# Attention probabilities turned by VectorE and DMA instead of TensorE, with four engines in the program's order

## The chip, the core and the metric

One NeuronCore of a Trainium2 chip runs the whole program. The metric is the device time of one execution in microseconds; three runs of the kernel before gave 835.94, 836.59 and 836.82 us, a median of 836.59. A profile of one execution shows when each instruction ran on TensorE (PE), VectorE (DVE), ScalarE (ACT) and GpSimd (POOL); SyncE (SP) issues DMAs.

## The reference

Two layers on 512 tokens of width 1024, each behind an RMS norm and added to the residual, and a final RMS norm: a state-space mixer (layer 0), then latent attention with 16 heads (layer 1), which the change touches. Cut to that:

```python
proj = u @ in_w
c_q, c_kv, k_r, z = proj[..., :384], proj[..., 384:640], proj[..., 640:704], proj[..., 704:]
q = (rms_norm(c_q, q_norm_w) @ uq_w).reshape(bsz, seq, 16, 192)
kv = (rms_norm(c_kv, kv_norm_w) @ ukv_w).reshape(bsz, seq, 16, 128 + 128)
q_full = concat([q[..., :128], rope(q[..., 128:])])
k_full = concat([kv[..., :128], rope(k_r) for every head])
s = einsum('bqhd,bkhd->bhqk', q_full, k_full) * 192 ** -0.5       # causal
o = einsum('bhqk,bkhd->bqhd', softmax(s), kv[..., 128:])
y = (o.reshape(bsz, seq, 2048) * silu(z)) @ out_w
return rms_norm(h + y, final_norm_w)
```

## The kernel before

All is float32. For accuracy each operand of a large matmul is kept as a high part, rounded to the fast format (`a`, `qh`, `ph`, `whi`, written by a ScalarE cast), and a rest (`b`, `ql`, `pl`, `wlo`, written by a VectorE subtraction that reads the high part); a product is three matmuls, the last with one of the rests. So each tile that feeds TensorE passes ScalarE and then VectorE.

Layer 0 (`ssm`, up to some 425 us of the span) is the same in both kernels. `mla` then computes the first projection, norms, and the 16 heads.

- `front_a(j)` and `front_b(j)` project q, k, v and the rope part for heads 2j and 2j+1. `front_a` runs under even heads (with rope: three VectorE steps, two ScalarE casts and two VectorE rests; the two halves of the rope tile are swapped by four DMAs into `rsw`), `front_b` under odd heads (with v). `zgemm(i)` projects the gate of head i.
- `score(h, b)` multiplies q-block b (128 tokens) with all keys up to it, takes the masked minimum on VectorE, the exponential with its sum on ScalarE, then the reciprocal and the scaling on VectorE: probabilities p, with queries on partitions.
- `turn(h, kb)` brings keys onto partitions: one 128x128 transpose on TensorE for each query block from kb on (4 + 3 + 2 + 1 per head, L817), then the cast `ph` (L821) and the rest `pl` (L822).
- `product(h, kb)` multiplies v with them: (va, ph), (vb, ph), (va, pl), 512, 384, 256 and 128 wide. After the fourth the result is multiplied with the gate.
- `zsilu(m)` applies the silu to four gates; ScalarE loads another function table before and the exponential's again after.
- `out_tok` multiplies with the output weights, for the first 8 heads while the last heads run.

What sets the order: TensorE's queue is the program's order. `sched(feed, pieces)` walks through the projections of a head (`feed`, which yields after about six matmuls with their cost) and puts in each score, turn and product once the fed cost passes its place; places are the tables SF (head 0's scores), SC (scores of head h+1 under head h), TU and PR (turns and products of head h), as shares of the head's cost. On all other engines a scheduler decides the order before. Every engine works through its queue in order: an instruction that waits holds up those behind it. Weights come through two raw buffers and three of each part; `weight` splits one weight ahead of the one in use (`LOOK`).

Of the kernel before, what the change touches and what calls it, by code (L numbers as in the profile page):

```python
# [15 lines left out]
P = 128  # L16
# [34 lines left out]
OA = 8  # L51
SQ = 2

# [98 lines left out]
class Net:  # L152
# [8 lines left out]
    def build(self):  # L161
# [18 lines left out]
        self.phase, self.group, self.before, self.head = "", [], [], None  # L180
        self.wq = []
        self.wpos = self.wload = 0
        self.wraws = []
        self.wready = {}
        for g in range(NG):
            for i in range(6):
                self.wq.append(("w", U_IN + 6 * g + i))
# [18 lines left out]
        with tc.tile_pool(name="ps_m", bufs=1, space=bass.MemoryType.PSUM, reuse_waits="tile") as ps, \  # L206
                tc.tile_pool(name="mla", bufs=2, reuse_waits="tile") as wk:
            self.ps, self.wk = ps, wk
            self.mla()

    LOOK = 1

    def link(self, ins, others):
        for o in others:
# [3 lines left out]
    def E(self, out, in_, func, **k):  # L218
        if self.phase != "E":
            pre = self.nc.scalar.preload_act_table_set("natural_log_exp_and_others")  # L220
            self.link(pre, self.group)
            self.phase, self.group, self.head = "E", [pre], pre
        i = self.nc.scalar.activation(out, in_, func, **k)  # L223
# [13 lines left out]
    def sched(self, feed, pieces=()):  # L237
        pieces = sorted(pieces, key=lambda p: p[0])
        done = 0.0
        for cost in feed:  # L240
            done += cost
            while pieces and pieces[0][0] <= done:
                pieces.pop(0)[1]()
# [3 lines left out]
    def weight(self, kind, idx):  # L247
        key = (kind, idx)
        self.prefetch(self.wq.index(key) + 1 + self.LOOK)
        return self.wready.pop(key)  # L250

    def prefetch(self, want):
        while self.wload < min(want + 1, len(self.wq)):
            self.wraws.append(self.load_weight(*self.wq[self.wload]))
            self.wload += 1
        while self.wpos < min(want, len(self.wq)):
            self.wready[self.wq[self.wpos]] = list(self.split_weight(self.wraws.pop(0)))[-1]
            self.wpos += 1

    def load_weight(self, kind, idx):  # L260
        n = {"w": 1024, "ua": 1024, "ub": 640, "uc": 512}[kind]
        raw = self.wraw.tile([P, n], F32, tag="raw", name=self.nm("raw"))
        self.nc.sync.dma_start(raw[:], self.t[kind][idx])
        return raw

    def split_weight(self, raw, cuts=()):
# [4 lines left out]
        for a, b in zip((0, *cuts), (*cuts, n)):  # L271
            nc.scalar.copy(hi[:, a:b], raw[:, a:b])  # L272
            nc.vector.tensor_tensor(lo[:, a:b], raw[:, a:b], hi[:, a:b].bitcast(F32), op=ALU.subtract)  # L273
# [29 lines left out]
    def run(self, g):  # L303
        for _ in g:
            pass
# [54 lines left out]
    def ssm(self):  # L360
# [45 lines left out]
        for i, w in enumerate(ws):  # L406
            self.wready[self.wq[i]] = next(w)
# [242 lines left out]
    def mla(self):  # L650
        tc, nc, t, wk = self.tc, self.nc, self.t, self.wk
        v = nc.vector
        self.bufs = {"b": 8}
        col = lambda i: self.cols[:, i:i + 1]
# [16 lines left out]
        for i in range(6):  # L671
# [6 lines left out]
            if i >= 2:  # L678
                for k in (2 * i - 4, 2 * i - 3):
                    ht = wk.tile([P, T], F32, tag=("ph", "pl")[k % 2], name=self.nm("ht"))  # L680
# [11 lines left out]
        def rope(raw):  # L692
# [11 lines left out]
        F = [{} for _ in range(8)]  # L704
# [10 lines left out]
        def zsilu(m):  # L715
            for i in range(4 * m, 4 * m + 4):
                self.S(zt[i][:], zt[i][:])

        def ksplit(src):
            k = wk.tile([P, 2, T], F32R, tag="k", name=self.nm("k"))  # L720
            nc.scalar.copy(k[:, 0], src)
            v.tensor_tensor(k[:, 1], src, k[:, 0].bitcast(F32), op=ALU.subtract)
            return k

        def front_a(j):
# [6 lines left out]
            rot = rope(raw)  # L732
            s1 = wk.tile([P, T], F32R, tag="s1", name=self.nm("s1"), bufs=1)
            s2 = wk.tile([P, T], F32R, tag="s2", name=self.nm("s2"), bufs=2)
            nc.scalar.copy(s1[lo, :], rot[lo, :])
            nc.scalar.copy(s2[hi, :], rot[hi, :])
            v.tensor_tensor(s1[hi, :], rot[lo, :], s1[lo, :].bitcast(F32), op=ALU.subtract)
            v.tensor_tensor(s2[lo, :], rot[hi, :], s2[hi, :].bitcast(F32), op=ALU.subtract)
            f["r", 0], f["r", 1] = s1, s2
# [3 lines left out]
            f["q", 0] = self.split(ps[:], "q", wk)  # L743
# [3 lines left out]
            f["k", 0] = ksplit(ps[:])  # L747
            yield 1.3

        def front_b(j):  # L750
# [4 lines left out]
            f["q", 1] = self.split(ps[:], "q", wk)  # L755
# [3 lines left out]
            f["k", 1] = ksplit(ps[:])  # L759
# [3 lines left out]
            for half in range(2):  # L763
# [13 lines left out]
                v.tensor_tensor(vb[:], ps[:], va[:].bitcast(F32), op=ALU.subtract)  # L777
# [3 lines left out]
        probs = [[] for _ in range(MH)]  # L781

        def score(h, b):
            f, i = F[h // 2], h % 2
            (qa, qb), kk = f["q", i], f["k", i]
# [285 lines left out]
```

## Time and profile before

| | us |
|---|---|
| the profiled execution | 836.13 |
| its span | 834.0 |
| busy in the span: TensorE, VectorE, ScalarE, GpSimd | 819.3, 644.9, 450.4, 0.2 |
| median of three runs | 836.59 |

The page says how long each engine was busy in the span of the execution; "idle before" a group is time in which its engine waited, and the name behind the arrow is what ended the wait. The granted clock of TensorE was 0.999 over the span. 50,856 DMA packets moved 90.55 MB, 21,552 of them under 512 bytes. All DMAs but a few are issued by SyncE.

### The profile page before, as it was taken

The page shows a single profiled execution, that of the slowest core. Times are in us where ns is not written, and L with a number is a line of the kernel's source. Part 1 is how long each engine was busy: PE and PEld are TensorE (multiplying, and loading weights), DVE is VectorE, ACT ScalarE, POOL GpSimd, SP SyncE. Part 2 cuts the span into 40 slices and gives each one's busy share as a digit, 9 for nine tenths or more (in the row PEclk, how much of TensorE's full clock was granted, in tenths as well). Part 3 has the DMA queues.
Part 4 walks back from the last instruction along what each step waited for, and adds up shares of the span by engine and source line. Part 5 has one row for each costly group of instructions (what it writes and reads, how often), then busy time and mean ns, then how long its engine had stood idle before and what let it go on. Part 6 is the DMA issues. An engine that isn't in the chain of part 4 may idle for free.

```text
span 834.0 us, 11549 instructions
## 1 busy us (share of the span) xinstructions
PE 819.3 (98%) x4228; PEld 691.8 (83%) x4228; DVE 644.9 (77%) x1234; ACT 450.4 (54%) x794; POOL 0.2 (0%) x4
## 2 busy tenths in 40 slices
PE   7999999999999999999999999999999999999996
PEld 5887888888888888888888888888888888888885
DVE  7999898979787989778566787786767869675544
ACT  7567755545465657434353654556547557554233
POOL 0000000000000000000000000000000000000000
PEclk9999999999999999999999999999999999999999
DMA  6364543423242423333555142222222224331212
GB/s 227 103 191 141 155 147 106 152 99 129 101 139 90 152 76 127 115 121 94 130 130 132 54 130 64 79 72 76 63 64 58 90 78 152 101 97 56 86 66 101
DMA packets 50856, 90.55 MB, mean 109 GB/s; under 512 B 21552, under 2 KB 23088, under 8 KB 50800
## 3 DMA queue, kind: packets, MB, share of 16 engines
q1 hardware_dynamic: 50080, 88.77, 34.0%
q10 hardware_dynamic: 720, 1.05, 0.3%
q8 instruction: 33, 0.54, 0.3%
q14 instruction: 23, 0.19, 0.1%
HBM read 83.12 MB, written 4.33 MB: 105 GB/s over the span
## 4 chain that ended last, share of the span: by engine, by line
PE 92%; DVE 3%; DMA 2%; ACT 1%; SPq 1%; issue 0%; DVEq 0%; ACTq 0%
PE mm L291 55%; PE ot L941 11%; PE s L793 5%; PE mm L300 4%; PE po L835 4%; PE mm L773 3%; PE pt L817 2%; PE yd L138 2%; PE yd L291 1%; PE aux L130 1%; PE aux L105 1%; DMA x<-in_x_dram 1%; PE aux L77 1%; PE aux L89 1%; DMA L<-ac_d 1%; DVE wlo L273 1%
## 5 line engine op out<-in xcount | busy, mean ns | idle before, releaser
L272 ACT CAST whi<-raw 128x1024 fp32r<-128x1024 f32 (+3 forms) x132 | 127.0, 965 | 210.3 <-PE mm L291 172.8
L273 DVE TENSOR_TENSOR wlo<-raw,whi 128x1024 fp32r<-128x1024 f32 (+3 forms) x132 | 146.8, 1115 | 54.6 <-ACT whi L272 54.3
L291 PE MATMUL mm<-ah,whi 128*128 128x512 f32 x384 | 154.0, 401 | 0.0
L291 PE MATMUL mm<-ah,wlo 128*128 128x512 f32 x384 | 150.3, 391 | 0.4 <-DVE wlo L273 0.4
L291 PE MATMUL mm<-al,whi 128*128 128x512 f32 x384 | 149.9, 390 | 0.0
L291 PE MATMUL mm<-vh,whi 128*128 128x512 f32 x224 | 89.4, 399 | 0.8 <-ACT whi L272 0.8
L291 PE MATMUL mm<-vh,wlo 128*128 128x512 f32 x224 | 87.9, 392 | 0.7 <-DVE wlo L273 0.7
L291 PE MATMUL mm<-vl,whi 128*128 128x512 f32 x224 | 87.6, 391 | 0.0
L291 PEld LDWEIGHTS mm<-ah,wlo 128*128 128x128 f32 x384 | 72.1, 188 | 16.1 <-DVE wlo L273 0.8
L291 PEld LDWEIGHTS mm<-ah,whi 128*128 128x128 f32 x384 | 72.2, 188 | 15.3 <-issue 1.4
L291 PEld LDWEIGHTS mm<-al,whi 128*128 128x128 f32 x384 | 72.2, 188 | 14.4 <-DVE al L312 0.3
L941 PE MATMUL ot<-whi,ah 128*128 128x512 f32 (+1 forms) x136 | 52.4, 385 | 0.0
L941 PE MATMUL ot<-whi,al 128*128 128x512 f32 (+1 forms) x136 | 51.5, 379 | 0.0
L941 PE MATMUL ot<-wlo,ah 128*128 128x512 f32 (+1 forms) x136 | 51.4, 378 | 0.0
L291 PEld LDWEIGHTS mm<-vh,wlo 128*128 128x128 f32 x224 | 42.1, 188 | 10.7 <-DVE wlo L273 1.5
L291 PEld LDWEIGHTS mm<-vh,whi 128*128 128x128 f32 x224 | 42.2, 188 | 9.4 <-ACT whi L272 1.1
L223 ACT ACTIVATE p<-p,st 128x128 f32<-128x128 f32 (+1 forms) x64 | 36.1, 564 | 25.3 <-DVE st L805 25.2
L291 PEld LDWEIGHTS mm<-vl,whi 128*128 128x128 f32 x224 | 42.2, 188 | 7.3
L821 ACT CAST ph<-pt 128x512 fp32r<-128x512 f32 (+1 forms) x64 | 26.4, 421 | 33.3 <-PE pt L817 32.8
L291 PE MATMUL mm<-ch,whi 128*128 128x512 f32 x104 | 42.6, 410 | 0.0
L291 PE MATMUL mm<-ch,wlo 128*128 128x512 f32 x104 | 40.9, 393 | 0.0
L291 PE MATMUL mm<-cl,whi 128*128 128x512 f32 x104 | 40.8, 392 | 0.0
(223 smaller groups left out, 1637.7 us busy)
## 6 DMA issues: line engine op xcount, KB each, us to landing
raw<-in_w_dram SPq DMA_DIRECT2D x100, 512.0 KB, 3.3
L<-ac_d SPq DMA_DIRECT2D x32, 256.0 KB, 3.9
E<-ea_d SPq DMA_DIRECT2D x32, 128.0 KB, 3.5
raw<-in_ua_dram SPq DMA_DIRECT2D x8, 512.0 KB, 3.3
raw<-in_ub_dram SPq DMA_DIRECT2D x8, 320.0 KB, 2.8
x<-in_x_dram SPq DMA_DIRECT2D x8, 256.0 KB, 4.4
res<-in_x_dram SPq DMA_DIRECT2D x8, 256.0 KB, 3.1
hd<-ht SPq DMA_DIRECT2D x32, 64.0 KB, 3.5
```

Source lines behind the costliest of these rows:

```text
L138: nc.tensor.matmul(yd[64 * h:64 * h + 64, s], self.xdt[j][:, c, h, :], self.L[2 * j + h][:, s], start=True, stop=True)
L223: i = self.nc.scalar.activation(out, in_, func, **k)
L272: nc.scalar.copy(hi[:, a:b], raw[:, a:b])
L273: nc.vector.tensor_tensor(lo[:, a:b], raw[:, a:b], hi[:, a:b].bitcast(F32), op=ALU.subtract)
L291: self.nc.tensor.matmul(ps, a, b, start=i == 0, stop=i == len(seq) - 1)
L300: self.nc.tensor.matmul(p, seq[i][0], seq[i][1], start=i == 0, stop=i == 3 * ks - 1)
L773: nc.tensor.matmul(ps[:, c2 * 256:(c2 + 1) * 256], a, b, start=i == 0, stop=i == 5)
L793: nc.tensor.matmul(ps[:, :n], x[:, s], y[:, :n], start=k == 0, stop=k == 4)
L817: nc.tensor.transpose(pt[:, (b - kb) * P:(b - kb + 1) * P], probs[h][b][:, kb * P:(kb + 1) * P], self.ident)
L821: nc.scalar.copy(ph[:, :n], pt[:, :n])
L835: nc.tensor.matmul(po[:, kb * P:], x, y, start=kb == 0 and k == 0, stop=kb == NCH - 1 and k == 2)
L941: nc.tensor.matmul(ps[:, a:b], x, y, start=start and i == 0, stop=stop and i == 5)
```

## The change

1. `turn` has no transposes. When a score's scaling is done, VectorE transposes the probabilities in blocks of 32x32 into `pb`, and SyncE writes `pb` with four DMAs (one per 32 partitions, in rows of 32 floats) to a DRAM tile `pd` so that it lies there turned. A new step `fetch(h)`, the fifth place of SF and SC, reads four blocks back into `pl`; `turn` casts `ph` from it, and the rest overwrites `pl` in place.
2. From the first scores on, VectorE, ScalarE, SyncE and GpSimd issue in the program's order too (`manual_schedule`). So that they don't stand in each other's way, many VectorE steps are recorded as `Later`: issued one or two ticks of the feed after they were due (`defer`, `tick`), or at once where somebody needs them (`now`).
3. Weights and the rope swaps are issued by GpSimd; SyncE keeps the probabilities, the residual and the output. SyncE follows the program's order from the start of `mla`. Weights are split two ahead.
4. All places are laid out anew; head 0's scores come among head 0's second front; `zsilu` has a place in the head (ZS), and output activations are cut earlier (`cut`, OA).

The diff, cut to its core:

```diff
-SF = (0.02, 0.1, 2.1, 3.1)
-SC = (0.0, 0.16, 0.25, 0.44)
-TU = (0.02, 0.08, 0.38, 0.55)
-PR = (0.3, 0.48, 0.65, 0.94)
-KO = (3, 4, 5, 8, 10)
+SF = (0.6, 1.0, 2.0, 3.2, 8.0)
+SC = (0.0, 0.1, 0.18, 0.28, 0.55)
+TU = (0.12, 0.22, 0.46, 0.66)
+PR = (0.28, 0.4, 0.66, 0.94)
+VB = 4.4
+ZS = 0.44
+KO = (4, 4, 4, 8, 10)
...
+    def defer(self, fn, lag=1):
+        e = Later(fn, lag)
+        if self.lagging:
+            self.later.append(e)
+        else:
+            e.now()
+        return e
...
+    def tick(self):
+        for e in list(self.later):
+            e.lag -= 1
+            if e.lag <= 0:
+                e.now()
+        self.later = [e for e in self.later if not e.done]
...
-        self.nc.sync.dma_start(raw[:], self.t[kind][idx])
+        self.wqueue.dma_start(raw[:], self.t[kind][idx])
...
-                nc.sync.dma_start(sw[32 * i:32 * i + 32, :], raw[32 * j:32 * j + 32, :])
+                nc.gpsimd.dma_start(sw[32 * i:32 * i + 32, :], raw[32 * j:32 * j + 32, :])
...
-            self.E(p[:], p[:], AF.Exp, scale=-1.0, bias=st[:, 0:1], accum_out=st[:, 1:2])
-            v.reciprocal(st[:, 2:3], st[:, 1:2])
-            v.tensor_scalar(p[:], p[:], st[:, 2:3], None, op0=ALU.mult)
-            probs[h].append(p)
+            p_exp = self.defer(functools.partial(
+                self.E, p[:], p[:], AF.Exp, scale=-1.0, bias=st[:, 0:1], accum_out=st[:, 1:2]))
+
+            def finish():
+                p_exp.now()
+                v.reciprocal(st[:, 2:3], st[:, 1:2])
+                v.tensor_scalar(p[:], p[:], st[:, 2:3], None, op0=ALU.mult)
+                pb = wk.tile([P, T], F32, tag="pb", name=self.nm("pb"))
+                v.transpose(pb[:, :n], p[:])
+                turned = pd[h % 2][:].rearrange("(j a) q -> a j q", a=32)
+                for i in range(4):
+                    q = b * P + 32 * i
+                    nc.sync.dma_start(turned[:, :n // 32, q:q + 32],
+                                      pb[32 * i:32 * i + 32, :n].rearrange("a (j q) -> a j q", q=32))
+
+            ends.append(self.defer(finish, 2))
...
+        def fetch(h):
+            while ends:
+                ends.pop(0).now()
+            for kb in range(NCH):
+                n = T - kb * P
...
+                pl = pl[:, :n]
+                nc.sync.dma_start(pl.bitcast(F32), pd[h % 2][kb * P:(kb + 1) * P, kb * P:])
+                back[h, kb] = pl
...
-            for b in range(kb, NCH):
-                nc.tensor.transpose(pt[:, (b - kb) * P:(b - kb + 1) * P], probs[h][b][:, kb * P:(kb + 1) * P],
-                                    self.ident)
...
-            nc.scalar.copy(ph[:, :n], pt[:, :n])
-            v.tensor_tensor(pl[:, :n], pt[:, :n], ph[:, :n].bitcast(F32), op=ALU.subtract)
-            parts[h].append((ph, pl))
+            nc.scalar.copy(ph[:, :n], pl.bitcast(F32))
+            e = self.defer(functools.partial(
+                v.tensor_tensor, pl, pl.bitcast(F32), ph[:, :n].bitcast(F32), op=ALU.subtract))
+            parts[h].append((ph, pl, e))
...
+        with self.tc.manual_schedule(engines={E.SP, E.DVE, E.Activation, E.Pool}):
+            self.lagging, self.look = True, 2
+            self.sched(chain(front_b(0), zgemm(4)), list(zip(SF, steps(0))))
...
+                if h and h % 4 == 0:
+                    pieces.append((ZS * cost, functools.partial(zsilu, h // 4)))
+                if h == 10:
+                    pieces.append((0.8 * cost, functools.partial(self.cut, zt, 0, 4)))
```

Two places show what the new order is. VectorE's queue in an even head (4), before: rope is `rraw` and `rsw`, `k` the rest of the keys, `pl` the rests for the third and fourth product, the ISA rows the masked minimum of the last score (`p`), `s_1066` and `s_1067` rope's rests.

```order
L697 TENSOR_TENSOR rraw_5383<-rraw_5383,con_3835 128x512
L698 TENSOR_TENSOR rsw_5385<-rsw_5385,con_3835 128x512
L722 TENSOR_TENSOR k_5444<-mm_5437,k_5444 128x512
L699 TENSOR_TENSOR rraw_5383<-rraw_5383,rsw_5385 128x512
L822 TENSOR_TENSOR pl_5455<-pt_5451,ph_5454 128x256
L805 ISA p_5477,st_5478<-s_5471,con_3835 128x512
L805 ISA st_5478 128x1
L737 TENSOR_TENSOR s_1066_5393<-rraw_5383,s_1066_5393 64x512
L738 TENSOR_TENSOR s_1067_5394<-rraw_5383,s_1067_5394 64x512
L807 RECIPROCAL st_5478<-st_5478 128x1
L822 TENSOR_TENSOR pl_5495<-pt_5492,ph_5494 128x128
L808 TENSOR_SCALAR p_5477<-p_5477,st_5478 128x512
```

The third product's rest stands ahead of the last score's minimum here. In the changed kernel, the same queue in the same head; the last score's minimum and the first two rope steps come just ahead of these rows, `p_5508` and `p_5528` are scores 2 and 3 of the next head, `wlo` a weight's rest:

```order
L745 TENSOR_TENSOR rraw_5469<-rraw_5469,rsw_5471 128x512
L886 RECIPROCAL st_5509<-st_5509 128x1
L887 TENSOR_SCALAR p_5508<-p_5508,st_5509 128x384
L889 STREAM_TRANSPOSE pb_5551<-p_5508 128x384
L64 TENSOR_TENSOR k_5542<-mm_5535,k_5542 128x512
L886 RECIPROCAL st_5529<-st_5529 128x1
L887 TENSOR_SCALAR p_5528<-p_5528,st_5529 128x512
L889 STREAM_TRANSPOSE pb_5578<-p_5528 128x512
L814 TENSOR_TENSOR s_1090_5547<-rraw_5469,s_1090_5547 64x512
L815 TENSOR_TENSOR s_1091_5548<-rraw_5469,s_1091_5548 64x512
L64 TENSOR_TENSOR wlo_5567<-raw_5434,whi_5566 128x512
L64 TENSOR_TENSOR pl_5400<-pl_5400,ph_5592 128x256
```

The third product's rest `pl_5400` is now behind all of them.

ScalarE's queue around the silus of gates 4 to 7, before; `z` are the gates, `ph_5368` and `ph_5376` the casts for the first two products of head 4, `p_5279` an exponential:

```order
L821 CAST ph_5303<-pt_5301 128x128
L223 ACTIVATE p_5279,st_5280<-p_5279,st_5280 128x512
L232 ACT_TABLE_LOAD
L232 ACTIVATE z_4584<-z_4584 128x512
L232 ACTIVATE z_4760<-z_4760 128x512
L232 ACTIVATE z_4954<-z_4954 128x512
L232 ACTIVATE z_5134<-z_5134 128x512
L220 ACT_TABLE_LOAD
L272 CAST whi_5460<-raw_5338 128x640
L821 CAST ph_5368<-pt_5363 128x512
L821 CAST ph_5376<-pt_5372 128x384
```

They stand at the seam between heads 3 and 4, after the last cast of head 3. In the changed kernel, the same silus; `k_5542` is the cast of the keys, `p_5528` the exponential of the last score, `s_1090` and `s_1091` rope's casts, `ph_5592` the cast for the third product of head 4:

```order
L774 CAST k_5542<-mm_5535 128x512
L258 ACTIVATE p_5528,st_5529<-p_5528,st_5529 128x512
L809 CAST s_1090_5547<-rraw_5469 64x512
L810 CAST s_1091_5548<-rraw_5469 64x512
L313 CAST whi_5566<-raw_5434 128x512
L267 ACT_TABLE_LOAD
L267 ACTIVATE z_4628<-z_4628 128x512
L267 ACTIVATE z_4818<-z_4818 128x512
L267 ACTIVATE z_5026<-z_5026 128x512
L267 ACTIVATE z_5220<-z_5220 128x512
L252 ACT_TABLE_LOAD
L921 CAST ph_5592<-pl_5400 128x256
```

They moved from the seam into head 4, ahead of its third product's cast.

More of the change, by code (lines that the diff above doesn't have):

```diff
@@ L690, in mla, with swap @@
                 cq.append(o)
-        def rope(raw):
+        def swap(raw):
             sw = wk.tile([P, T], F32, tag="rsw", name=self.nm("rsw"), bufs=1)
@@ L703, in mla, with settle @@
         zt = []
-        F = [{} for _ in range(8)]
+        F = [{"w": []} for _ in range(8)]
+        def settle(f):
+            for e in f["w"]:
+                e.now()
+            f["w"] = []
         def zgemm(i):
@@ L731, in front_a @@
             nc.scalar.copy(raw[:], ps[:])
[L732 to L739, printed above, removed]
+            sw = swap(raw)
             yield 0.2
@@ L861, in norm, with steps @@
             return hs, ls
+        def steps(h):
+            return [functools.partial(score, h, b) for b in range(NCH)] + [functools.partial(fetch, h)]
         outg = out0()
```

204 lines of the change are left out of this document (136 added, 68 removed).

## The prediction

> **What bounds the kernel now.** I read the page first, then the stretches of the attention part, then the chain that ended last inside one head.
>
> ```profile
> span 834.0 us, 11549 instructions
> PE 819.3 (98%) x4228; PEld 691.8 (83%) x4228; DVE 644.9 (77%) x1234; ACT 450.4 (54%) x794; POOL 0.2 (0%) x4
> ...
> 504.30:521.30 17.00, 17.00 (x91) 14.55 (x89) 13.18 (x33) 8.47 (x19) 0.00 (x0) 1.00 0.25 78
> 521.30:539.10 17.80, 17.80 (x106) 15.79 (x104) 12.78 (x31) 8.78 (x19) 0.00 (x0) 1.00 0.20 64
> ```
>
> The last two rows are one even and one odd head of the attention part (us; then busy us of PE, its weight loads, VectorE, ScalarE, GpSimd; granted clock; DMA share). TensorE is busy for every hundredth; VectorE has 3.8 and 5.0 us to spare. So work taken off TensorE is time, one for one, as long as nobody makes TensorE wait. The chain inside one even head (start us, us, what; mm = projections, pt = transposes, s = scores, po = products):
>
> ```profile
> 537.31 1.43 PE mm L291 x6
> 539.08 0.77 PE pt L817 x7
> 539.85 2.08 PE mm L291 x9
> 541.92 1.47 PE s L793 x10
> ...
> 545.47 0.69 PE po L835 x3
> ...
> 547.77 1.15 PE s L793 x5
> 548.92 0.52 PE po L835 x3
> ...
> L817 PE MATMUL pt<-ident,p 128*128 128x128 f32 x160 | 25.3, 273 | 0.0
> ```
>
> **What the change removes.** 160 transposes on TensorE. Their group (last row) shows 273 ns each, but that is the length of overlapping records; in the chain seven take 0.77 us, 0.11 each. 160 x 0.109 = 17.4 us, all on the path. The Trainium skill ("TensorE: Matmul & The Clock Gate", Part 4: PE-mode transpose) gives about 275 ns for one in a kernel; by that the saving would be 44 us and the forecast below about 819. The record agrees with that figure, the distance between starts doesn't, and it is the distance that counts.
>
> **What it adds on VectorE.** 64 block transposes, and the program's order in place of the scheduler's. Costs are distances from start to start, from an even head of before:
>
> ```profile
> 544.97 0.42 DVE L808 TENSOR_SCALAR p<-p,st 128x384 f32<-128x384 f32 x1
> 545.30 0.68 DVE L312 TENSOR_TENSOR ql<-mm,qh 128x512 fp32r<-128x512 f32 x1
> 545.93 0.69 DVE L273 TENSOR_TENSOR wlo<-raw,whi 128x512 fp32r<-128x512 f32 x1
> 546.54 0.69 DVE L697 TENSOR_TENSOR rraw<-rraw,con 128x512 f32<-128x512 f32 x1
> 547.14 0.69 DVE L698 TENSOR_TENSOR rsw<-rsw,con 128x512 f32<-128x512 f32 x1
> 547.74 0.68 DVE L722 TENSOR_TENSOR k<-mm,k 128x512 fp32r<-128x512 f32 x1
> 548.35 0.68 DVE L699 TENSOR_TENSOR rraw<-rraw,rsw 128x512 f32<-128x512 f32 x1
> 548.95 0.42 DVE L822 TENSOR_TENSOR pl<-pt,ph 128x256 fp32r<-128x256 f32 x1
> 549.28 0.68 DVE L805 CUSTOM_DVE_ANT_0 p<-s,con 128x512 f32<-128x512 f32 x1
> ...
> 550.00 0.69 DVE L737 TENSOR_TENSOR s<-rraw,s 64x512 fp32r<-64x512 f32 x1
> 550.72 0.69 DVE L738 TENSOR_TENSOR s<-rraw,s 64x512 fp32r<-64x512 f32 x1
> 551.43 0.16 DVE L807 RECIPROCAL st<-st 128x1 f32<-128x1 f32 x1
> ...
> L681 DVE STREAM_TRANSPOSE ht<-res x8: 699/711/712, 388.2 to 431.6; 128x512 f32<-128x512 f32 x8
> L684 SPq DMA_DIRECT2D hd<-ht x32: 341/487/856, 389.0 to 448.9; - x32
> hd<-ht SPq DMA_DIRECT2D x32, 64.0 KB, 3.5
> hr<-hd SPq DMA_DIRECT2D x8, 256.0 KB, 2.9
> rsw<-rraw SPq DMA_DIRECT2D x32, 64.0 KB, 2.0
> ```
>
> A 512-wide transpose lasts 0.71, about 0.63 from start to start (neighbours of 0.69 stand 0.61 apart); 384 wide, by the slope between 256 (0.33) and 512 (0.61), 0.47. Four per head are some 1.7 us: 13.2 + 1.7 of 15.9 us in an even head. VectorE stays under TensorE in sum. What decides is the place in its queue.
>
> An even head now, in us from its first matmul, TensorE unhindered: up to the third product stand 36 projection matmuls (36 x 0.231 = 8.3), scores (0.34, up to 539.08, + 1.47 + 1.15) and two products (0.69 + 0.52): 12.5. The product's third matmul, at 12.75, needs the rest `pl`. The last score (18 matmuls 4.2 + scores 2.96) is done at 7.15. Behind it VectorE has, ahead of that `pl`: the masked minimum 0.60, three rope steps 1.80, finishing score 2 (0.08 + 0.33 + 0.47), k's rest 0.61, finishing score 3 (0.08 + 0.40 + 0.63; 0.40 is the 512-wide scaling), rope's two rests 1.43, the weight's rest 0.61, and `pl` itself 0.33: 7.4, so 14.55. TensorE waits 1.8 us, where before `pl` stood ahead of the last score and nobody waited. An odd head has no rope: from its start VectorE holds, by the same distances, an estimated 12.3 us of work up to that `pl` and idles some 0.7, 13.0 against a need at 13.5: no wait, though with half a us of cover.
>
> **The silus on ScalarE.** In heads 4, 8 and 12 four silus with a table load on each side now stand between the weight's cast and the cast `ph` for the third product.
>
> ```profile
> 549.06 0.62 ACT L735 CAST s<-rraw 64x512 fp32r<-64x512 f32 x1 [2.22 <-DVE rraw L699]
> 549.71 0.62 ACT L736 CAST s<-rraw 64x512 fp32r<-64x512 f32 x1
> 550.35 0.72 ACT L223 ACTIVATE p<-p,st 128x512 f32<-128x512 f32 x1
> ...
> 568.74 1.28 ACT L232 ACT_TABLE_LOAD   x1
> 570.03 2.19 ACT L232 ACTIVATE z<-z 128x512 f32<-128x512 f32 x4
> 572.24 1.28 ACT L220 ACT_TABLE_LOAD   x1
> 573.53 0.73 ACT L272 CAST whi<-raw 128x640 fp32r<-128x640 f32 x1
> ```
>
> ScalarE can't begin them early: the cast of k ahead of them waits for the k projection, 24 matmuls, all scores and one product into the head (9.2). Then k 0.55 (512-wide casts last 0.62 here, less what overlaps), the exponential 0.72, rope's casts 1.29, the weight 0.55: 12.3. The block lasts 573.53 - 568.74 = 4.8, `ph` 0.25: 17.3, against a need at 12.5. TensorE waits 4.8 us. In head 12 two more casts (0.53 each) stand ahead: 5.8. Before, the same block lay at the end of the head before (these rows), with no work due behind it.
>
> **Round trip, queues, ends.** Turning now goes by DRAM: after the transpose four writes 0.49 apart (1.5), 3.5 to land, SyncE waiting for them, then a read of 2.9: 7.9 at most, and 6.4 if a write lands in 2.0 as a swap does, since weights no longer stand ahead on that queue. An odd head's last transpose ends about 12.7, so the read lands 2.4 to 3.9 into the even head. ScalarE's next work there is the rope copy at 3, so the queue shifts by 0 to 1.3; I take 0, and 1.3 widens the range. Head 0 has 2 us less ahead of it, so there I take a shift of 1.2: its wait is 3.0 (2 to 5). In head 11 four rests of output activations (4 x 0.61) come ahead: 2.4 less 0.5 of cover and some idle time, 1.3. The first scores of all are moved ahead of head 0's second front; they need rope's rests and k's (1.43 + 0.61 = 2.0): wait 0 to 2, taken as 1. In heads 13 to 15 eight reads of the residual stand ahead of the last write of head 14 on SyncE: 0 to 4, taken as 1, since some 16 us lie between last score and first product. Weights and rope's swaps move to GpSimd's queue; the trace has no DMA there. On SyncE a swap lands in 2.0; bounds are 0 (weights are two steps ahead; swaps have 0.7 of cover) and 2.0 per even head, one swap's landing again; I take 0, for the cover. The prologue and the state-space part keep their work: 0, plus or minus 0.5.
>
> **Sum.** Waits: 1.0 first scores, 3.0 head 0, 3 x 1.8 heads 2, 6, 10, 2 x 4.8 heads 4 and 8, 5.8 head 12, 1.3 head 11, 1.0 end: 27.1. The profiled execution took 836.13 (its span of 834.0 and 2.1 around it): 836.13 - 17.4 + 27.1 = 845.8. The median of the runs is 0.46 above that execution: 846.3. About 0.2% (1.7 us) is what a measurement of this kernel can tell from no change.
>
> **Rivals.**
> *The saving wins (faster).* Its place is the same third product: if ScalarE gets to the silus with less ahead, or VectorE keeps pace, even heads wait about 0.5 instead of 1.8 and silu heads 3 instead of 5: with the ends 3.5, 4 x 0.5 + 3 x 3 + 3.5 = 14.5, so 833.7; with no such wait at all 836.6 - 17.4 + 3.5 = 822.7. It decides at 17.4 us of waits, 2.5 per even head. For it: sums of busy time leave room on every engine. Against: the queue ahead of `pl` is fixed by the program, and the k projection alone sets 9.2 + 0.5 + 4.8. Chance 0.17.
> *No change.* Waits of 16 to 19 us, 835 to 838: 0.07.
> *Transfers bind.* Swaps on GpSimd land 2 us later in seven even heads, or 128-byte rows and weights collide on the DMA engines (share now 0.20 to 0.25, about doubled) and the first product waits too: up to 14 more, 852 to 860. For it: odd heads have half a us of cover. Against: SyncE and the engines have the room. Chance 0.14.
> *TensorE slows after its waits.* At the start of the program ten matmuls take 4.5 us:
>
> ```profile
> 4.79 0.80 PE L300 MATMUL mm<-vh,whi 128*128 128x512 f32 x1 [4.79 <-ACT whi L272]
> ...
> 9.29 0.39 PE L300 MATMUL mm<-vl,whi 128*128 128x512 f32 x1
> ```
>
> That is 0.45 each against 0.231 later, 2.2 lost behind 4.8 us of idling. If a 4.8 us wait does this again in heads 4, 8 and 12, it costs 6.6: 853. For it: same length of idling. Against: it may be the first start alone that is slow; the granted clock shows 1.00 in both rows of the heads. Chance 0.12.
> By the Trainium skill ("TensorE: Matmul & The Clock Gate", Part 1: The HAM clock gate) an idle window of some 3.4 us halves the array's clock until a window of work has passed; by that rule this rival would hold in about two waits of five.
>
> **Numbers.** Forecast 846.3, its own stretch 839 to 852: 0.50. Faster 0.17, same 0.07, slower 0.50 + 0.14 + 0.12 = 0.76. Range 830 to 860: below it lie faster cases with two thirds of their chance (0.12), above it the two slow rivals together (0.05).
>
> **What would show it.** In the profile after: a projection and product step of 0.11 less per transposed block; TensorE idle in front of the third product of even heads, ended by `pl` on VectorE (1.8) and in heads 4, 8 and 12 by `ph` on ScalarE (4.8), with silus and table loads just ahead of it; odd heads dense at about 16.7. It is wrong if TensorE is as dense as before (then 819 to 823), if the waits stand ahead of first products and end with the read from DRAM, or if even heads last under 16.5.

## The result and the profile after

The changed kernel takes 901.21 us (median of four runs, 899.36 to 901.90) against 836.71 for the kernel before on the same chip: 1.0763 times as long, 95% interval 1.0736 to 1.0789. Slower was forecast, but by 10 us, not by 64. The profiled execution has a span of 899.7 us, 65.7 more than before.

From the page of the changed kernel; the last row is the granted clock in 40 slices of the span:

```profile
span 899.7 us, 11886 instructions
PE 829.9 (92%) x4068; PEld 690.4 (77%) x4068; DVE 675.3 (75%) x1298; ACT 448.4 (50%) x794; POOL 50.5 (6%) x100
...
PEclk9999999999999999999999989999898989889998
```

TensorE has 160 instructions fewer and is busy 10.6 us longer; six slices from the 24th to the 36th, where the heads run, show a lower clock (the seventh, at the very end, lies behind the last matmul). Both are signs of slow matmuls. The view of TensorE's waits (us in total, times, longest) names the rest of it:

```profile
PE po L938 <- ACT ph L921: 30.1, 9, 6.5
PE po L938 <- DVE pl L64: 21.1, 14, 3.1
```

Neither row exists before. With two small ones TensorE waits 52.9 us in the attention part, where it waited 0.3. Added up from start to start with waits left out, the same matmuls take 25.2 us more, and the transposes are 13.6 us less: 52.6 + 25.2 - 13.6 = 64.2 at the last matmul, and 1.6 more behind it.

The third product of head 2 in the timeline (start us, us; idle before, and what ended it), VectorE and the matmuls that wait for it:

```profile
556.40 0.52 DVE L880 CUSTOM_DVE_ANT_0 p<-s,con 128x384 f32<-128x384 f32 x1
557.92 0.68 DVE L880 CUSTOM_DVE_ANT_0 p<-s,con 128x512 f32<-128x512 f32 x1
...
559.13 0.68 DVE L744 TENSOR_TENSOR rsw<-rsw,con 128x512 f32<-128x512 f32 x1
559.85 0.69 DVE L745 TENSOR_TENSOR rraw<-rraw,rsw 128x512 f32<-128x512 f32 x1
...
562.18 0.14 DVE L886 RECIPROCAL st<-st 128x1 f32<-128x1 f32 x1
562.36 0.49 DVE L887 TENSOR_SCALAR p<-p,st 128x512 f32<-128x512 f32 x1
...
562.84 0.39 PE L938 MATMUL po<-ph,va 128*128 128x256 f32 x1 [1.29 <-ACT ph L921]
562.88 0.71 DVE L889 STREAM_TRANSPOSE pb<-p 128x512 f32<-128x512 f32 x1
...
563.62 0.69 DVE L814 TENSOR_TENSOR s<-rraw,s 64x512 fp32r<-64x512 f32 x1
564.34 0.69 DVE L815 TENSOR_TENSOR s<-rraw,s 64x512 fp32r<-64x512 f32 x1
565.06 0.69 DVE L64 TENSOR_TENSOR wlo<-raw,whi 128x512 fp32r<-128x512 f32 x1
565.67 0.62 DVE L64 TENSOR_TENSOR pl<-pl,ph 128x256 fp32r<-128x256 f32 x2
...
566.14 0.58 PE L938 MATMUL po<-pl,va 128*128 128x256 f32 x1 [2.81 <-DVE pl L64]
```

The rest `pl` is last in the row that the prediction listed, and TensorE waits 1.29 + 2.81 = 4.1 us, not 1.8. Two things add. The steps that hang on one another (rope's third, the scaling behind the reciprocal, the transpose behind it) stand further apart than neighbours do: from the minimum's start to `pl`'s start it is 7.75 us, where the prediction's steps add up to 7.04. And the row begins late: the last score is through at 556.2, its minimum starts at 557.92. The cause is at the head's begin on ScalarE:

```profile
553.20 0.62 ACT L921 CAST ph<-pl 128x512 fp32r<-128x512 f32 x1 [3.90 <-DMA pl<-pd]
553.73 0.58 ACT L791 COPY rraw<-mm 128x512 f32<-128x512 f32 x1
```

ScalarE stands 3.9 us before the first cast, until the turned block is back from DRAM, with rope's copy and the first exponentials behind it, and VectorE behind these.

The silus of head 4 on the chain of waits, with what follows on TensorE:

```profile
600.41 0.62 ACT whi L313
...
601.04 1.28 ACT L267
...
602.87 1.65 ACT z L267 x3
...
604.54 1.28 ACT L252
...
605.84 0.41 ACT ph L921
...
606.29 1.04 PE po L938 x3
607.33 4.02 PE mm L333 x12
```

The block lasts 4.8 us as forecast, and the wait is 5.6. The last row is new: twelve projection matmuls take 4.02 us, where at full speed they take 2.8. The end of head 15, on the same chain:

```profile
819.09 6.07 DMA pd<-pb
...
825.43 4.07 DMA pl<-pd
...
829.58 0.63 ACT ph L921
...
830.25 1.65 PE po L938 x3
```

The last writes of head 15's probabilities take 6.07 us to land, the reads 4.07, and TensorE waits 5.4 us.

### The profile page after: what moved, and what is told of

Same layout as the page of the kernel before. It is cut to its first block, busy times and chain, and to the rows that moved or that the text cites. A ratio compares the mean times of both kernels' runs of the same rounds, so it can differ in the third digit from the quotient of the medians.

```text
span 899.7 us, 11886 instructions
## 1 busy us (share of the span) xinstructions
PE 829.9 (92%) x4068; PEld 690.4 (77%) x4068; DVE 675.3 (75%) x1298; ACT 448.4 (50%) x794; POOL 50.5 (6%) x100
## 4 chain that ended last, share of the span: by engine, by line
PE 61%; DVE 17%; DMA 9%; ACT 7%; issue 4%; SPq 2%; POOL 0%; ACTq 0%; DVEq 0%
PE mm L333 41%; PE ot L1053 6%; PE mm L342 4%; DMA pd<-pb 3%; DMA pl<-pd 3%; DVE wlo L64 2%; PE yd L150 2%; PE po L938 2%; DVE p L887 2%; DVE p L880 1%; PE yd L333 1%; DVE pl L64 1%; PE aux L142 1%; SPq L893 1%; DMA x<-in_x_dram 1%
## 5 line engine op out<-in xcount | busy, mean ns | idle before, releaser
L333 PE MATMUL mm<-vh,whi 128*128 128x512 f32 x224 | 92.6, 414 | 1.0 <-ACT whi L313 1.0
L333 PE MATMUL mm<-vh,wlo 128*128 128x512 f32 x224 | 91.7, 410 | 1.2 <-DVE wlo L64 1.2
L333 PE MATMUL mm<-vl,whi 128*128 128x512 f32 x224 | 91.6, 409 | 0.0
L1053 PE MATMUL ot<-whi,al 128*128 128x512 f32 (+1 forms) x136 | 54.3, 399 | 0.0
L304 POOL DMA_DIRECT2D raw<-in_w_dram x36 | 19.5, 541 | 600.9 <-DMA hd<-ht 417.9
L333 PEld LDWEIGHTS mm<-vh,whi 128*128 128x128 f32 x224 | 45.1, 201 | 10.4 <-ACT whi L313 1.2
L64 DVE TENSOR_TENSOR pl<-pl,ph 128x512 fp32r<-128x512 f32 (+1 forms) x64 | 29.8, 477 | 30.3 <-ACT ph L921 30.3
L938 PE MATMUL po<-ph,va 128*128 128x512 f32 (+1 forms) x64 | 22.1, 345 | 30.1 <-ACT ph L921 30.1
L921 ACT CAST ph<-pl 128x512 fp32r<-128x512 f32 (+1 forms) x64 | 28.2, 453 | 41.5 <-DMA pl<-pd 41.5
L938 PE MATMUL po<-pl,va 128*128 128x512 f32 (+1 forms) x64 | 24.3, 379 | 21.1 <-DVE pl L64 21.1
```

The source lines that it names most:

```text
L64: self.fn()
L304: self.wqueue.dma_start(raw[:], self.t[kind][idx])
L333: self.nc.tensor.matmul(ps, a, b, start=i == 0, stop=i == len(seq) - 1)
L921: nc.scalar.copy(ph[:, :n], pl.bitcast(F32))
L938: nc.tensor.matmul(po[:, kb * P:], x, y, start=kb == 0 and k == 0, stop=kb == NCH - 1 and k == 2)
L1053: nc.tensor.matmul(ps[:, a:b], x, y, start=start and i == 0, stop=stop and i == 5)
```

## The experiments

My theory after this: what TensorE waits for is the place of a step in the queues of VectorE and ScalarE (A), and each wait of some 2 us or more is paid again as slow matmuls. Against it stood, in various forms, that turning by VectorE and DMA is too slow in any order (B).

**Silus later.** `-ZS = 0.44` `+ZS = 0.72`

> One number is changed: ZS 0.44 to 0.72, so that in heads 4, 8 and 12 the four silus and their two table loads stand behind ScalarE's casts of the third and fourth turned block instead of ahead of them. Theory A (what TensorE waits for is the place in the queues of VectorE and ScalarE, and each long wait is followed by slow matmuls): the wait of 5.6, 5.8 and 6.5 us at the third product falls to what heads 2, 6 and 10 show without silus (4.1, 4.6, 3.7), since the rest pl then comes late on VectorE: 5.5 us less, the slow matmuls stay, 901.2 becomes 896 (893 to 899). Theory B (the silus alone make these heads late): the third product of heads 4, 8 and 12 waits under 1 us and the slow matmuls behind it go too (3 x 2.3): 901.2 - 15 - 7 = 879 (876 to 883). Theory C (the turned blocks come too late through DRAM, wherever ScalarE's work stands): within 3 us of 901.2.

Measured: 890.17 us, 1.0628 [1.0612, 1.0644] of before (837.27). TensorE waits 45.3 us, at the third products of heads 4, 8 and 12 4.8, 3.8 and 4.9, now mostly for `pl` on VectorE. So A: the silus only hid a second wait. It fell 6 us further than A said: eight stretches of slow matmuls were left, not ten, and head 15's wait of 5.4 was gone.

**Turned blocks cast earlier.** `-TU = (0.12, 0.22, 0.46, 0.66)` `+TU = (0.12, 0.22, 0.32, 0.44)`

> TU is changed from (0.12, 0.22, 0.46, 0.66) to (0.12, 0.22, 0.32, 0.44): the cast ph and the rest pl of the third and fourth turned block are put ahead of the silus on ScalarE and ahead of the last score's masked minimum and of rope's steps on VectorE. Theory A (place in the queues): the waits at the third product of heads 0, 2, 6, 10 (18.7 us) and 4, 8, 12 (17.9) go, and with them seven of the ten stretches of slow matmuls (19.8 of 25.7 us): 901.2 - 56.4 = 845 (840 to 852); left are head 11, the end and odd heads' 0.4 each. Theory B (VectorE, ScalarE and the way through DRAM cannot carry the turning in the time of a head, whatever the order): the waits come back at other products and at the scores, 880 or more. Between: silus and rope then make something else late (the exponentials, hence the next head's first product): 855 to 875.

Measured: 885.42 us, 1.0576 [1.0554, 1.0598]. The number is B's, the place isn't. VectorE in head 2 of this run:

```profile
559.85 0.69 DVE L814 TENSOR_TENSOR s<-rraw,s 64x512 fp32r<-64x512 f32 x1
560.57 0.69 DVE L815 TENSOR_TENSOR s<-rraw,s 64x512 fp32r<-64x512 f32 x1
561.28 0.42 DVE L64 TENSOR_TENSOR pl<-pl,ph 128x256 fp32r<-128x256 f32 x1
```

The same product waits 2.7 us in all seven even heads from 0 to 12, for a rest that is still put off behind rope's rests; the silus' waits are gone. The edit hadn't done what I meant.

**The new order, turning on TensorE.** The block transposes, writes and reads are taken out of the changed kernel, and `turn` has the 160 transposes of the kernel before.

> The order, tables and queues of the changed kernel, but the probabilities are turned by 160 transposes on TensorE as before: no block transposes, no way through DRAM. Theory A (the order laid anew makes the waits, turning by VectorE and DMA only some of them): third products of even heads wait about 1.2 us less each (block transposes of 0.47 and 0.63 ahead of pl are gone), silu heads still wait 5 or more, the waits of 11 us in heads 13 to 15 go with the writes and reads, and 13.6 us of transposes come back: 901.2 + 13.6 - 7 x 1.2 - 10 - 5 (slow matmuls of the end) = 891 (880 to 900). Theory B (turning itself makes the waits): nearly all waits and slow matmuls go: 836 to 850.

Measured: 871.02 us, 1.0397 [1.0380, 1.0415], between the two. The waits that are left (23.0 us) are at the places of A: 4.7, 4.7 and 5.8 with silus, 1.0 in heads 0, 2, 6 and 10. So the order alone costs 34 us; turning by VectorE and DMA in that order costs another 30, although it takes 13.6 us of transposes away.

**A wait put in by hand.** In the kernel before, at the end of eight heads (`m` copies of 128 x `n`):

```
+gz = wk.tile([P, T], F32R, tag="gz", bufs=1)
+nc.gpsimd.tensor_copy(gz[:, :n], zt[h][:, :n])
+for _ in range(m - 1): nc.gpsimd.tensor_copy(gz[:, :n], gz[:, :n])
+nc.tensor.matmul(dz[:, :128], gz[:, :128], gz[:, :128])
```

> The kernel before, with a wait put in by hand at the end of eight heads: GpSimd copies a tile made from the head's output one to eight times, and one small matmul (its result is not used) has to wait for it, so that TensorE idles for different lengths, read from the trace. Nothing else is changed. Theory A (TensorE slows after a wait, and the length of the wait decides): behind the longer waits, from some 2 to 3 us on, ten to sixteen matmuls start 0.43 us apart instead of 0.23, 2 to 3.5 us lost behind each; behind the shorter none. The time is 836.7 plus the waits plus 2 to 3.5 for each long wait. Theory B (the slow matmuls of the changed kernel come from its traffic on VectorE and the DMA queues, not from the wait): all matmuls stay at 0.23, and the time is 836.7 plus the waits, within 1.

Measured: 890.23 us in one run. The waits were 2.19, 2.71, 2.46, 3.87, 4.74, 4.96, 5.92 and 10.28, together 37.1. Behind the first nothing slows; behind the second, 0.5 us longer, everything does:

```profile
539.88 0.33 PE L913 MATMUL dz<-gz 128*128 128x128 f32 x1 [2.19 <-POOL gz L909]
...
540.34 0.39 PE L292 MATMUL mm<-cl,whi 128*128 128x512 f32 x1
540.57 0.39 PE L292 MATMUL mm<-ch,wlo 128*128 128x512 f32 x1
540.79 0.39 PE L292 MATMUL mm<-ch,whi 128*128 128x512 f32 x1
```

```profile
559.93 0.47 PE L913 MATMUL dz<-gz 128*128 128x128 f32 x1 [2.71 <-POOL gz L909]
...
560.73 0.63 PE L292 MATMUL mm<-cl,whi 128*128 128x512 f32 x1
561.16 0.63 PE L292 MATMUL mm<-ch,wlo 128*128 128x512 f32 x1
561.59 0.63 PE L292 MATMUL mm<-ch,whi 128*128 128x512 f32 x1
```

Starts are 0.23 apart in the first, 0.43 in the second, and the granted clock says the same: 1.00 from 540.3 to 543.3, 0.50 from 560.2 to 562.8. All seven waits from 2.46 up were followed by such a stretch; the starts add up to some 15.2 us more than before, 2.2 per wait (half the time worked at clock 0.50: 1.6 behind the wait of 2.71, 2.9 behind the one of 10.28). So A, with no way through DRAM and no traffic of the change in the kernel.

The traces' record of the granted clock also shows which waits do it. The clock is 1.00 or 0.50, and it changes only on a grid of 3.41 us (here at 559.65, 563.06, 583.54, 586.95). Taking all runs' attention parts together: of the grid steps at full clock in which TensorE stood idle for 1.81 us or more, all 62 were followed by a step at 0.50; of those with 0.5 to 1.56 us, none of 128; in between, 3 of 13. So where a wait falls counts as much as its length: 2.19 us split by the grid into 1.47 and 0.72 cost nothing more, 2.46 split into 0.61 and 1.85 did.

**Rests of the third block first.** `+TU = (0.14, 0.22, 0.285, 0.42)`, and in `turn`: `+if kb == 2: e.now()`

> In the run with TU moved, the cast ph of the third block went ahead of the silus, but its rest pl was still put off by one step of the feed, and so stood behind rope's five VectorE steps and both finishing scores: heads 0, 2, 6 and 10 kept 2.7 us. Now TU = (0.14, 0.22, 0.285, 0.42), and the third block's rest is issued at once, ahead of rope. Theory A (place in VectorE's queue): the third product's wait is under 0.5 us in heads 2, 4, 6, 8, 10 and 12, and their slow matmuls go; left are the first scores (1.6), part of head 0 (1.5), head 11 and odd heads (3) and the end (12, with 2 to 3 slow stretches, 7): 836.7 - 13.6 + 18 + 7 = 848 (842 to 856). Theory B (too much VectorE work or too long a way through DRAM, whatever the order): the wait moves to the fourth product, the scores or the next head's first product, and the time stays over 870.

Measured: 850.02 us, 1.0163 [1.0146, 1.0180]. VectorE in head 2, where the rest now stands ahead of rope:

```profile
548.98 0.68 DVE L880 CUSTOM_DVE_ANT_0 p<-s,con 128x512 f32<-128x512 f32 x1
549.59 0.08 DVE L880 DVE_READ_ACCUMULATOR2_ANT st<- 128x1 f32 x1
549.59 0.42 DVE L64 TENSOR_TENSOR pl<-pl,ph 128x256 fp32r<-128x256 f32 x1
549.92 0.69 DVE L743 TENSOR_TENSOR rraw<-rraw,con 128x512 f32<-128x512 f32 x1
```

51 us of the 64 are gone by the place of one VectorE step and the casts around it (earlier casts without that step had given 16), 33 of them waits and 18 slow matmuls: A. No third product waits any more, two slow stretches are left of ten. 20 us of waits remain, among them about 1.2 at each fourth product of an even head (2.35 in head 12) and 6.7 at the first product of head 14.

**The residual's reads.** `-nc.sync.dma_start(r[m][:], hd[...])` `+nc.gpsimd.dma_start(...)`, on that kernel and alone:

> The kernel with the third rest first, and the eight reads of the residual (hr, 256 KB each) are issued on GpSimd's queue instead of SyncE's, where they stood between the writes of head 14's turned probabilities. Theory A (the write waits behind these 2 MB on its own queue): the waits at the first product of heads 14 and 15 (5.4 us in the changed kernel, 7.2 and 4.5 in the run with TU moved) go, with one or two slow stretches: 5 to 14 us under the run without this edit. Theory B (the reads take the DMA engines from the write on any queue): within 3 us of it.

> The changed kernel, and only the eight reads of the residual go to GpSimd's queue. Theory A: head 15's wait for ph of 5.4 us and the 12 slow matmuls behind it (2.3 us) go, the end's waits on VectorE (3.1, 0.9, 1.5) stay: 901.2 - 7.7 = 893.5 (890 to 897). Theory B (the DMA engines, not the queue): within 3 us of 901.2. Theory C (everything that waits at the end is late by VectorE anyway, and the wait is only moved): 898 to 903.

Measured: 847.40 us (1.0124 [1.0109, 1.0139]), 2.6 less, which is B's number, and 894.64 (1.0696 [1.0666, 1.0726]), 6.6 less, which is A's; but the traces show neither as it was meant.

In the first run head 14's wait fell from 6.7 to 3.1, by about half: its last four writes landed in 5.1 to 5.7 us, not 6.4 to 8.1. A queue of its own takes part of the delay away, and the rest stays. The Trainium skill ("DMA: Bandwidth & Descriptors", Queues, rings and completion order) says that a DMA engine takes turns between the queues that have work, a packet at a time; by that rule a write on another queue no longer stands behind all of the reads, but still shares with them, and this run agrees.

In the second run head 15's wait fell from 5.4 to 2.5, but not beside the residual: in the changed kernel the residual has landed by 801 us, and head 15's last writes are issued from 817 on. What runs beside them is a 512 KB weight read, in both kernels (the last write takes 6.1 us to land, then 5.0); the run with the silus later had lost this wait with the residual still on SyncE. All waits together fell by only 1.5 us. The rest of the gain is seven slow stretches instead of ten, which cost 15.7 us instead of 22.5: 1.72 us in head 11 in both kernels, and 3.13 against 3.22 us in head 13, were followed by clock 0.50 in the changed kernel and not here, where the grid cut them into 1.54 and 0.18, and 1.73 and 1.49; head 15's 2.49 us fell on two steps as well. That is mostly luck, not the queue.

**More steps put ahead.** On the kernel with the third rest first: `+if kb >= 2: e.now()`, `-self.defer(rests, 2)` `+self.defer(rests, 3)`; and in the first of the two also the residual's reads on GpSimd's queue, one ahead of each step of weight 2, and `+OA = 4` with two splits in head 10.

> The kernel with the third rest first, and further: the fourth block's rest is issued at once too, rope's rests one step later; the residual is read on GpSimd's queue, one tile ahead of each step of output weight 2 and of its counterpart in the second half, not eight at once; the splits of the first eight outputs are spread (two in head 10, four in head 11, two in head 12). Theory A (only order and the placing of transfers cost; the turning itself is covered): the waits at the fourth products (6 x 1.2), in heads 11 and 12 (3.2) and in front of head 14's first product (6.7) go, with the two slow stretches behind the longest (7): 850 - 24 = 826 (822 to 833), faster than the kernel before. Theory B (VectorE is full in even heads, so that each step put ahead makes another late): the waits move to the scores or the next head's products, 838 to 850.

> Of that kernel only the first part: the fourth block's rest at once, rope's rests one step later; the residual's reads and the outputs' splits stay as in the changed kernel. Theory A: the 1.2 us at the fourth product of the even heads go, and the 2.35 of head 12 with its slow stretch falls: 850 - 8 = 842 (838 to 845). Theory B: VectorE is full, and the waits are only moved: 847 to 853.

Measured: 853.98 (1.0186 [1.0159, 1.0213]) and 859.01 (1.0263 [1.0243, 1.0283]): misses, slower than without. Fourth products wait less, but first products of heads 1, 3, 5 and 7 wait 1.0 to 2.2 us; in the first run head 15 also waits 8.8 for reads that run beside the residual's, in the second there are five slow stretches. The transfers in the second of these kernels, at the seam of heads 2 and 3: issue on GpSimd's queue, on SyncE's, and the median us to landing:

```profile
558.49 0.54 POOL L304 DMA_DIRECT2D raw<-in_ua_dram  x1 [8.26 <-DVE pl L64]
```

```profile
548.68 11.03 SPq L893 DMA_DIRECT2D pd<-pb  x16
564.51 2.01 SPq L914 DMA_DIRECT2D pl<-pd  x4
```

```profile
raw<-in_ua_dram POOLq DMA_DIRECT2D x1, 512.0 KB, 5.1
...
pd<-pb SPq DMA_DIRECT2D x4, 64.0 KB, 4.5
```

The last writes are issued up to 559.7; a 512 KB weight read started at 558.49, and they took 4.5 us to land. In the run with only the third rest first they took 1.9. Putting rope's rests off had moved the weight's rest, which frees the buffer for that read, ahead: 1.4 us on VectorE, the length of rope's rests, decided a collision on the DMA engines.

**Fourth rest ahead of the finishing.** `+TU = (..., 0.405)`, `if kb >= 2`, rope's rests as before; residual read on SyncE behind the reads of heads 13 and 14; splits spread. And the same with `-self.wqueue = nc.gpsimd` `+self.wqueue = nc.sync`:

> In the last two runs a 512 KB weight read started 1 us into the last four writes of head 2's turned probabilities, and these took 4.5 us to land, not 1.9; so head 3's first product waited. Now, on the kernel with the third rest first: the fourth block is cast and its rest issued right behind the second product, ahead of the last finishing (TU[3] 0.405), rope's rests and the weight's rest stay where they were; the residual is read on SyncE behind the reads of heads 13 and 14 (four tiles each), no longer between the writes; the splits of the first outputs are spread. Theory A (order, and which transfers run beside a turn's last writes): fourth products wait under 0.4 us, heads 12 and 14 under 1, odd heads' first products none: 850 - 6 - 2 - 6 - 7 (slow matmuls) = 829 (825 to 835). Theory B (the collision comes back wherever VectorE's steps move by a microsecond): first products of odd heads wait 1 to 2 us again, 840 to 855.

> The same kernel with one line changed: in the attention part the weights are read on SyncE's queue again, as before the change, in one row with the writes and reads of the turned probabilities; rope's swaps stay on GpSimd. Theory A (a second queue lets a weight read run over the last writes; in one row it cannot): no write lands later than 2.5 us, but the read of the turned block stands behind the weight read, some 2 us: within 4 us of the run without this line. Theory B (a weight read that waits for its buffer blocks SyncE's row): writes and reads of the turned blocks start late, first products of most heads wait 2 us or more, and the time is 15 or more above it.

Measured: 848.93 (1.0149 [1.0123, 1.0175]) and 888.72 (1.0625 [1.0602, 1.0647]). The first is B: no fourth product waits any more, but first products do, 1.5 to 2.5 us in heads 0, 4, 5 and 9, 1.0 in head 14 and 6.0 in head 15. The second is B by size, for another reason in part: 15 of its 45.5 us of waits are for weights ahead of head 0, which no longer arrive in time. A queue of its own for weights is a gain in this order, in spite of collisions.

**Turning taken out of the mended order, and put back for some heads.** On that kernel, `VIA` names the heads that are turned by VectorE and DMA, the others are turned by TensorE: `VIA = ()` and `VIA = (2, 4, 6, 8, 10, 12)`. The blocks that come back from DRAM now lie in the buffers that odd heads used before.

> The mended order (third and fourth rest at once, TU 0.14, 0.22, 0.285, 0.405, residual read behind the reads of heads 13 and 14, splits spread), but the probabilities of all heads turned by transposes on TensorE; no writes to or reads from DRAM for them. Theory A (what the mended order still loses, some 12 us at TensorE's end, is the way through DRAM, collisions with weight reads and the end): no first product waits, 13.6 us of transposes come back, left are the first scores (1.6) and some steps of under 1: 836.9 + 4 = 841 (837 to 845). Theory B (the program's order itself loses it, on VectorE and ScalarE): waits of 12 us or more stay and the transposes come on top, 850 to 862.

> The same kernel, but heads 2, 4, 6, 8, 10 and 12 are turned by VectorE and DMA (their scores stand in odd heads, where VectorE has no rope to do), the other ten by TensorE. Six heads give 6 x 0.85 = 5.1 us of transposes. Theory A (a way through DRAM is covered where VectorE has room and no residual is read): 5 us under the run with all transposes on TensorE (3 to 6). Theory B (each way through DRAM meets a weight read and makes the next first product late, 1 to 2.5 us per head): equal to that run or up to 8 above it.

Measured: 842.16 (1.0064 [1.0052, 1.0076]) and 841.94 (1.0066 [1.0054, 1.0079]). The first is A: 3.5 us of waits are left, no slow stretch. So of the 12 us that the mended order lost with all turning through DRAM, 7 were the way through DRAM, transposes saved included, and 5.5 the order. The second is neither: 4.6 us of transposes less, 4.4 of waits more, of these 3.2 around head 12, where its turning stands beside its silus and the outputs' splits (that these are the cause was not tested by itself). The last two runs: `+SF = (1.6, 2.0, 3.0, 4.2, 8.0)`, `+OA = 3`, the last half of the output out of the program's order, `VIA = ()` and `VIA = (2, 4, 6, 8, 10)`.

> The mended order with all turning on TensorE, and three more places: the first scores one step of the feed later (SF from 1.6), the splits of the outputs spread as three, two, two and one, and the last output's half issued as the scheduler orders it, not in the program's order (the time from the last matmul to the end was 8.9 us, 7.3 in the kernel before). Theory A (what this order loses against the kernel before is at these places): 842.2 - 0.8 - 1.5 - 1.5 = 838.4 (836.5 to 840). Theory B (the program's order loses a little everywhere): 841 to 843.

> The same, with heads 2, 4, 6, 8 and 10 turned by VectorE and DMA: 5 x 0.85 = 4.3 us of transposes less, and waits of 1.1 at rests in front of products, as the run with six such heads showed for these five (its 4.4 us in heads 11 and 12 came with the sixth). Theory A (turning so pays where VectorE has room and nothing else is read): 3 us under the run without it, 835.4 (833.5 to 837.5), as fast as the kernel before or a little faster. Theory B (it never pays): equal to that run or above.

Measured: 839.06 (1.0037 [1.0023, 1.0051]) and 835.00 (0.9983 [0.9974, 0.9992]). From the page of the last:

```profile
span 834.2 us, 11672 instructions
PE 814.8 (98%) x4178; PEld 684.7 (82%) x4178; DVE 656.3 (79%) x1254; ACT 449.1 (54%) x794; POOL 50.6 (6%) x100
...
PEclk9999999999999999999999999999999999999999
```

A in both: turning five heads whose scores stand in odd heads is worth 4 us by the medians, 2.9 by the spans of the two profiled executions. This is the only version that is not slower than the kernel before. It is 1.6 us faster by the medians, no more than the 1.7 us that the prediction called the least it could tell, and its interval ends just under 1.

## Why the prediction was wrong

The places of the waits were mostly right. Three terms of the sum failed: the shift of the queues behind the way through DRAM, taken as 0; the end, taken as 1.0; and the slowing of TensorE behind its waits, which was left out of the sum.

- **The saving** was sized at 17.4 us from one row (0.11 per transpose); the starts of all 160 give 13.6 (0.085). A small miss, and on the slow side.
- **The silus** went as worked out: the block lasts 4.8, ends with the cast `ph`, and costs 5.6, 5.8 and 6.5 us of waits (forecast 4.8, 4.8, 5.8). The run with later silus showed what the forecast lacked: behind them the late `pl` was waiting, so that moving them gains 4 us of 18.
- **Heads 2, 6 and 10**: 4.1, 4.6 and 3.7, not 1.8. The place was right, and the run with that rest first proved it. The failed step is "the queue shifts by 0 to 1.3; I take 0": in even heads up to 12 the block's way back took 7.0 to 8.6 us from the last transpose to the cast, with ScalarE waiting for it (forecast 6.4 to 7.9). In head 2 it landed 4 us into the head, in front of rope's copy, and shifted VectorE by 1.7. The other 0.7 is distances from start to start taken from neighbours that don't hang on one another. Head 0 (6.3, not 3.0) shows the same waits; odd heads up to 9 waited 0.4 each where their half a us of cover was taken as enough.
- **The end**: 11.0 us, not 1.0. In heads 13 and 14 (5.6 together) the rest `pl` came late on VectorE: in head 13 the splits of the outputs stand ahead of the last scaling. In head 15 (5.4) the turned block came late. From the last transpose to the cast it took 12.9 us in head 14, whose last writes share the DMA engines with the 2 MB of residual (5.4 to 6.4 us to land), and 12.6 in head 15, whose last writes meet a weight read (6.1). "Some 16 us lie between last score and first product" left these out.
- **The rival that should have been in the sum**: TensorE slows after its waits. It had the mechanism, the price (2.2 us, measured 2.3 on average, 1.4 to 3.0 each) and a chance of 0.12; it counted three places. There were ten. The same matmuls took 25.2 us more, 22.5 of it at clock 0.50: half of what the waits and slow matmuls cost together beyond the forecast's 27.1. By the rule that the prediction quoted (the Trainium skill, "TensorE: Matmul & The Clock Gate", Part 1: The HAM clock gate), an idle window of some 3.4 us is needed. The trace agrees with the length of the window (steps of 3.41 us) and with the halving, but not with a whole idle window: 1.81 us of idling in a step was always enough. So "two waits of five" was too little: every wait of 3.9 us or more in these runs was followed by slow matmuls.
- **Transfers bind** had a chance of 0.14 and up to 14 us: right in kind at the end and wherever a weight read meets a last write, about 7 us in the mended order.

In sum: for 27.1 us of waits 52.9, for 0 of slow matmuls 25.2, for 17.4 saved 13.6, and a tail 1.6 longer: 901. What is not settled: what decides in a step with between 1.57 and 1.80 us of idling, where 3 of 13 were followed by the low clock.

## What to carry to other kernels

When an order is laid down by the program, list for each operand that the bounding engine waits for what stands ahead of it in its queue, and put the small rest that frees the next product ahead of the work that nobody is waiting for: here one step and its casts were worth 51 us of 64. In these runs a wait of TensorE that filled 1.81 us or more of one 3.41 us step of the clock's grid was paid twice, once as itself and once as 1.4 to 3.1 us of matmuls at half clock, so several middling waits cost more than one long one; before a gain is put down to an edit, count these stretches. Work moved off the bounding engine through DRAM paid here only for some heads, and was slower wherever its last writes met another transfer; take it head by head, not everywhere.

## What the runs showed of the hardware

TensorE's granted clock was 1.00 or 0.50 and changed only on a grid of 3.41 us. A step at full clock with 1.81 us or more of idling was followed by one at 0.50 (62 of 62), one with 0.5 to 1.56 us was not (0 of 128). At 0.50, matmuls of 128 x 512 start 0.43 us apart, 0.23 otherwise; behind a wait of 10.28 us this cost 2.9 us, behind one of 2.71 us 1.6. Four writes of 64 KB in rows of 128 bytes landed in 1.9 us alone and in 4.5 with a 512 KB read beside them on another queue. VectorE's third rope step (128 x 512), which reads what the step before it wrote, starts 0.72 us behind it; steps of this size that read nothing of each other stand 0.60 to 0.61 apart. Rope's two rests of 64 x 512 stand 0.72 apart too, though neither reads the other.
